# Sums of weights made during attention, each load and first add tied to a converted weight unit by a one-column Pool operation

## The chip, the core and the metric

The kernel runs on one core of one Trainium2 chip. The metric is the device time of one execution in microseconds (us); before the change its median is 2242.68 us in three runs.

## What is computed

Two layers of a transformer trunk, over 256 tokens of 2048 features, in float32. Each layer mixes the tokens with two groups of heads that read the same `x`, adds and normalises, and then runs a SwiGLU network with 5632 hidden features:

```
proj = x @ w_in                      # 5008 columns, split into qa, ka, va, qi, wi, ki, cq, ckv, kr
out_a = top-64 sparse attention(rope(qa), rope(ka), va), keys chosen by an indexer on qi, ki, wi
out_b = latent attention(rms(cq) @ w_uq, rms(ckv) @ w_ukv, rope(kr))
x = layer_norm(ALPHA * x + concat(out_a, out_b) @ w_o) * ln1_g + ln1_b
h = silu(x @ w_gate) * (x @ w_up)
x = layer_norm(ALPHA * x + h @ w_down) * ln2_g + ln2_b
```

## The kernel before

**Weights.** Nearly all of the work of TensorE (PE) is float32 products with weights, which come from HBM in units of 128 x 1024 numbers (512 KB; block TB's have 800 columns in place of 1024). SyncE (SP) issues the load of a unit into a tile `raw` (L309, four buffers in the attention phase). `parts` then makes two halves of it that together hold the full precision: ScalarE (ACT) copies it to `wh` in the rounded format (L327), VectorE (DVE) takes the difference `wl` (L328), and the buffers of `wh` and `wl` come round every five units. PE multiplies 12 times with a unit of 1024 columns, in L349, L350 and L351: two tiles of tokens, two slices of 128 rows, three products each.

**Stages of a layer.** First the blocks of the input projection, eight units each: QI0, TA, QI1, TB, then KA0, with the indexer running beside them; the latent queries (2 + 4 units), QA0, VA0, 4 units, KA1, QA1, VA1, and the output projection `w_o` (24 units, then a last pass). Attention heads are worked off between the units. Then comes the network: eleven chunks of 512 hidden features, of which the later ones multiply by a scheme with seven products in place of eight and need sums of weight units.

**Sums made ahead.** For the chunks 4 to 10 one set of these sums is made during attention, by the generator `presums`. For each chunk it loads four units into tiles `q` (four buffers) through the queue of GpSimd (Pool, L761), and DVE makes four adds and subtractions of them (L770, L771, L773, L774). The four results go back to HBM through Pool's queue (L779), from where the network stage reads them. `presums` runs once a layer, and is spawned after block TB.

**What sets the order.** The code is written as generators that say after how many ticks they go on: `tick` is called after nearly every weight unit. From the code's order a scheduler then makes one list of instructions for each engine; an operation that nothing holds back can stand in that list far ahead of its place in the code. Engines and DMA queues work strictly in the order of their lists, and wait with semaphores for each other. From the spawn of `presums` to the end of the 24 units of `w_o` there are 82 ticks, and `finish(early)` behind them runs off what is left of it.

**Other users of Pool's queue.** At the start of a layer the norm of TB's outputs uses it: the loads of `gq` and `gk` (L602, L603), and small operations `rve` and `rrs` (L585, L587) of which DVE waits in `rn` (L588). The phase after attention reuses the memory of `q`, so the first load of that phase waits for all stores of the sums.

Of the kernel before, what the change touches and what calls it, by code (L numbers as in the profile page):

```python
# [24 lines left out]
F32 = mybir.dt.float32  # L25
# [3 lines left out]
ALU = mybir.AluOpType  # L29
# [3 lines left out]
P = 128  # L33
# [49 lines left out]
def hybrid_trunk(ctx: ExitStack, tc: tile.TileContext, x, xt_in, pos, w_in, g_cq, g_ckv, w_uq,  # L83
                 w_ukv, w_o, ln1_g, ln1_b, ln1_T, w_gu, w_down, ln2_g, ln2_b, ln2_T, out):
    nc = tc.nc
# [7 lines left out]
    def nm(s):  # L93
        uid[0] += 1
        return f"{s}{uid[0]}"
# [16 lines left out]
    def pt(shape, dt, s, tag=None, bufs=1):  # L112
        assert phase["name"] == "att"
        return phase["pool"].tile(shape, dt, name=nm(s), tag=tag or s, bufs=bufs)
# [36 lines left out]
    def f(ap):  # L151
        return ap.bitcast(F32)
# [20 lines left out]
    mhalf = const.tile([P, 1], F32, name="mhalf")  # L173
# [22 lines left out]
    def rope_tables():  # L196
# [14 lines left out]
        magic = 1.5 * 2.0 ** 23  # L211
        two_pi = 2.0 * math.pi
        parts, rest = [], two_pi
        for bits in (8, 8, 8):
            e = math.floor(math.log2(rest)) + 1 - bits
# [82 lines left out]
    def some(key, have, more):  # L298

        if phase["name"] == "more":  # L300
            phase[key] = phase.get(key, 0) + 1
            if phase[key] * more % (have + more) < more:
                return phase["pool"], more
        return sb, have
# [7 lines left out]
    def load_sum(a, b):  # L312
# [3 lines left out]
        nc.gpsimd.dma_start(raw, b, accum_op=ALU.add)  # L316
        return raw

    def parts(raw, n, own=None):

        if own is not None:
            wh, wl = own[:, 0], own[:, 1]
        else:
            pool, bufs = some("n", UNITS, MORE)
            wh = pool.tile([P, KU * C], F32R, name=nm("wh"), tag="wh", bufs=bufs)
            wl = pool.tile([P, KU * C], F32R, name=nm("wl"), tag="wl", bufs=bufs)
        nc.scalar.activation(wh[:, :n], raw[:, :n], AF.Copy)  # L327
        nc.vector.tensor_tensor(wl[:, :n], raw[:, :n], f(wh[:, :n]), op=ALU.subtract)  # L328
        return wh[:, :n].rearrange("p (k c) -> p k c", k=KU), wl[:, :n].rearrange("p (k c) -> p k c", k=KU)

    def load_unit(src, n):

        return parts(load_raw(src, n), n)
# [188 lines left out]
    def layer(l, xh, xl, norms, last):  # L522
# [231 lines left out]
        def presums():  # L754

            for fc in range(ALLFROM, NFC):
                u = EARLY

                def load(i, v):
                    d = pt([P, KU * C], F32, "q", bufs=4)  # L760
                    nc.gpsimd.dma_start(d, w_gu[i][l, fc, v])  # L761
                    return d

                b12, b22 = load(1, u), load(1, u + HALF)
                yield 1
                b11 = load(0, u)
                yield 1
                b21 = load(0, u + HALF)
                yield 3
                nc.vector.tensor_tensor(b12, b12, b22, op=ALU.add)  # L770
                nc.vector.tensor_tensor(b11, b12, b11, op=ALU.add)  # L771
                yield 1
                nc.vector.tensor_tensor(b22, b11, b22, op=ALU.subtract)  # L773
                nc.vector.tensor_tensor(b21, b11, b21, op=ALU.add)  # L774
                yield 1
                ready[fc] = {}
                for i, (name, v) in enumerate((("p7", b12), ("p6", b11), ("p5", b22), ("p4", b21))):
                    d = hbm.tile([P, KU * C], F32, name=nm("q"), tag=f"{l}_{fc}_{name}", bufs=1)
                    nc.gpsimd.dma_start(d, v)  # L779
                    ready[fc][name] = d  # L780
                    if i % 2:
                        yield 2

        def aff(c):
            if l:
# [29 lines left out]
        if l == 0:  # L815
            load_x()
        early = spawn(presums())
        ka, p_ka = dsa_qk(KA0)
        finish(p_tb)
# [38 lines left out]
        def last_pass(unit, ks, lhs, then):  # L858

            us = []  # L860
            two = many([P, 2, 2, KU * C])
            for c in range(D // C):
                own = two[:, c] if c < 2 else t8([P, 2, KU * C], F32R, "own")
                us.append([load_unit(unit(c, ks[0]), KU * C), parts(load_raw(unit(c, ks[1]), KU * C), KU * C, own)])
            for t in range(NT):
                for c in range(D // C):
                    o = acc()
                    for i, k0 in enumerate(ks):
                        wh, wl = us[c][i]
                        for j in range(KU):  # L870
                            h, lo = lhs(t, k0 + j)
                            mm(o, h, wh[:, j, :], start=i == 0 and j == 0, stop=False)
                            mm(o, h, wl[:, j, :], start=False, stop=False)
                            mm(o, lo, wh[:, j, :], start=False, stop=i == len(ks) - 1 and j == KU - 1)
                        tick()
                    sl = xt[t][:, c * C:(c + 1) * C]
                    with tc.high_priority(offset=SOON):
                        nc.vector.tensor_tensor(sl, sl, o, op=ALU.add)
                then(t)
# [320 lines left out]
```

## Time and profile before

| | before |
|---|---|
| runs (3) | 2241.27 to 2244.99 us, median 2242.68 |
| the profiled execution | 2243.01 us; span 2241.2 us, mean granted clock 0.984 |
| PE busy | 2153.5 us (96%) |
| DVE busy | 1848.8 us (82%) |
| ACT busy | 1292.5 us (58%) |
| Pool busy | 215.0 us (10%) |
| DMA | 552.97 MB, mean 247 GB/s |

The time of the profiled execution is 1.8 us longer than its span, the stretch from the first to the last profiled instruction. A stretch A:B is given in us from the start of the span. In a list of operations the columns are start, duration, engine, line, operation, tiles written<-read, shape; in square brackets is the idle time of the engine just before and what ended it. "issue" there means that nothing in the profile shows what was waited for. Matmuls are pipelined, so that the durations of neighbours overlap: the distance of their starts, not their duration, is what one costs. PEclk is the share of full clock granted to PE. The lines of a helper (L309, L327 and so on) gather all its callers.

### The profile page before, as it was taken

Reading aid. Unit: us, or ns where it says so; the run is one execution under the profiler, and the core shown is the slowest. Engines: PE = TensorE matmul, PEld = TensorE weight load, DVE = VectorE, ACT = ScalarE, POOL = GpSimd, SP = SyncE. Lnnn points to the kernel's source line nnn. Section 1 sums busy time; section 2 is a strip of 40 time slices with the busy share of each in tenths; the row PEclk is TensorE's granted clock in tenths of the full one; section 3 lists DMA queues with packets and bytes.
Section 4 is the critical chain, followed back from the end, with each engine's and each line's share of the span. In section 5 each row is a group of like instructions: output and inputs, shape, how many; then the busy total and the mean of one; then the engine's idle time right before and its main releaser. Section 6 shows DMA issues by size and latency. Waiting matters only on the chain.

```text
span 2241.2 us, 28348 instructions
## 1 busy us (share of the span) xinstructions
PE 2153.5 (96%) x9948; PEld 1779.4 (79%) x9948; DVE 1848.8 (82%) x2361; ACT 1292.5 (58%) x1675; POOL 215.0 (10%) x368
## 2 busy tenths in 40 slices
PE   7869999999999999999997799999999999999997
PEld 5758888888888878878886688888888888878886
DVE  5578556799989999999666876668999899999996
ACT  4345545466666666667453455545656666666663
POOL 2220000000011010000112200000000101101101
PEclk9989999999999999999998899999999999999999
DMA  9976546667888998987759865585678889889894
GB/s 313 377 269 214 162 157 228 200 214 231 244 244 267 275 280 270 281 274 243 243 216 345 296 203 170 185 264 173 220 255 234 244 275 270 268 264 281 274 321 125
DMA packets 158833, 552.97 MB, mean 247 GB/s; under 512 B 17905, under 2 KB 18209, under 8 KB 158049
## 3 DMA queue, kind: packets, MB, share of 16 engines
q1 hardware_dynamic: 119808, 431.15, 55.4%
q0 software_dynamic: 38736, 119.87, 21.1%
q8 instruction: 78, 1.28, 0.2%
q14 instruction: 67, 0.54, 0.1%
q10 hardware_dynamic: 144, 0.13, 0.0%
HBM read 498.12 MB, written 31.46 MB: 236 GB/s over the span
## 4 chain that ended last, share of the span: by engine, by line
PE 72%; issue 9%; DVE 9%; DMA 8%; POOL 1%; ACT 1%; POOLq 0%; DVEq 0%; ACTq 0%
PE acc L350 14%; PE acc L349 14%; PE acc L351 14%; DVE wl L328 4%; PE gu_p L971 4%; PE gu_p L972 4%; PE gu_p L969 4%; DMA raw<-in_w_up_dram 3%; PE gu_c L972 2%; PE gu_c L969 2%; PE gu_c L971 2%; PE tr L369 2%; DMA q<-q 2%; DMA q<-in_w_up_dram 2%; PE att L972 1%
## 5 line engine op out<-in xcount | busy, mean ns | idle before, releaser
L327 ACT ACTIVATE wh<-raw 128x1024 fp32r<-128x1024 f32 (+1 forms) x910 | 939.5, 1054 | 683.6 <-PE acc L351 247.3
L328 DVE TENSOR_TENSOR wl<-raw,wh 128x1024 fp32r<-128x1024 f32 (+1 forms) x910 | 1079.6, 1214 | 217.7 <-ACT wh L327 213.4
L349 PE MATMUL acc<-wh,xh 128*128 128x512 f32 (+1 forms) x768 | 307.4, 401 | 6.8 <-ACT wh L327 6.7
L350 PE MATMUL acc<-wl,xh 128*128 128x512 f32 (+1 forms) x768 | 302.4, 394 | 9.1 <-DVE wl L328 9.1
L351 PE MATMUL acc<-wh,xl 128*128 128x512 f32 (+1 forms) x768 | 301.4, 393 | 0.0
L350 PE MATMUL acc<-wl,hT 128*128 128x512 f32 x640 | 250.5, 391 | 0.4
L349 PE MATMUL acc<-wh,hT 128*128 128x512 f32 x640 | 249.4, 390 | 0.0
L351 PE MATMUL acc<-wh,hT 128*128 128x512 f32 x640 | 249.3, 390 | 0.0
L349 PEld LDWEIGHTS acc<-wh,xh 128*128 128x128 f32 x768 | 147.8, 192 | 39.7 <-ACT wh L327 8.9
L350 PEld LDWEIGHTS acc<-wl,xh 128*128 128x128 f32 x768 | 147.6, 192 | 39.2 <-DVE wl L328 13.0
L351 PEld LDWEIGHTS acc<-wh,xl 128*128 128x128 f32 x768 | 147.2, 192 | 28.8 <-DVE xl L415 0.6
L350 PEld LDWEIGHTS acc<-wl,hT 128*128 128x128 f32 x640 | 120.1, 188 | 29.8 <-DVE wl L328 5.3
L349 PEld LDWEIGHTS acc<-wh,hT 128*128 128x128 f32 x640 | 120.2, 188 | 25.2
L969 PE MATMUL gu_c<-wh,xh 128*128 128x512 f32 x360 | 140.2, 389 | 0.0
L972 PE MATMUL gu_c<-wh,xl 128*128 128x512 f32 x360 | 140.1, 389 | 0.0
L971 PE MATMUL gu_c<-wl,xh 128*128 128x512 f32 x360 | 140.1, 389 | 0.0
L351 PEld LDWEIGHTS acc<-wh,hT 128*128 128x128 f32 x640 | 120.2, 188 | 24.5
L316 POOL DMA_DIRECT2D sum<-in_w_up_dram x56 | 47.9, 855 | 902.0 <-DMA sum<-in_w_up_dram 414.7
L1082 POOL DMA_DIRECT2D x<-d x80 | 68.8, 891 | 488.8 <-ACT d L1081 478.4
L971 PE MATMUL gu_p<-wl,many 128*128 128x512 f32 x240 | 94.6, 394 | 7.5 <-DVE wl L328 7.5
L972 PE MATMUL gu_p<-wh,many 128*128 128x512 f32 x240 | 93.5, 390 | 0.0
L969 PE MATMUL gu_p<-wh,many 128*128 128x512 f32 x240 | 93.5, 389 | 0.0
(294 smaller groups left out, 3680.3 us busy)
## 6 DMA issues: line engine op xcount, KB each, us to landing
raw<-in_w_gate_dram SPq DMA_DIRECT2D x176, 512.0 KB, 6.5
raw<-in_w_down_dram SPq DMA_DIRECT2D x176, 512.0 KB, 7.9
raw<-in_w_in_dram SPq DMA_DIRECT2D x144, 512.0 KB, 4.6
raw<-in_w_up_dram SPq DMA_DIRECT2D x106, 512.0 KB, 5.5
raw<-in_w_o_dram SPq DMA_DIRECT2D x64, 512.0 KB, 4.6
q<-q POOLq DMA_DIRECT2D x56, 512.0 KB, 5.5
sum<-in_w_up_dram SPq DMA_DIRECT2D x56, 512.0 KB, 3.7
sum<-in_w_up_dram POOLq DMA_DIRECT2D x56, 512.0 KB, 8.7
```

Source lines behind the costliest of these rows:

```text
L316: nc.gpsimd.dma_start(raw, b, accum_op=ALU.add)
L327: nc.scalar.activation(wh[:, :n], raw[:, :n], AF.Copy)
L328: nc.vector.tensor_tensor(wl[:, :n], raw[:, :n], f(wh[:, :n]), op=ALU.subtract)
L349: mm(o[t][:, :n], h, a, start=first, stop=False)
L350: mm(o[t][:, :n], h, b, start=False, stop=False)
L351: mm(o[t][:, :n], l, a, start=False, stop=final)
L369: nc.tensor.transpose(psum[:, i * P:(i + 1) * P], s, ident)
L969: mm(o[name], h, a, start=name not in begun, stop=False)
L971: mm(o[name], h, b, start=False, stop=False)
L972: mm(o[name], l, a, start=False, stop=end)
L1082: nc.gpsimd.dma_start(xt[t][:, c * C:(c + 1) * C], d, accum_op=ALU.add)
```

## The change

Three things change, in `parts`, `presums` and a new helper.

- `parts` remembers the `wh` tile that it last handed out (`latest["wh"]`).
- Ahead of each load of `presums`, a Pool operation writes the first column of the tile to be loaded, from the first column of that `wh`. The load overwrites the tile afterwards; so it has to wait for the operation, and the operation for the conversion of that unit.
- Ahead of the first add of each chunk, a Pool operation reads the first columns of `b12` and of the latest `wh` into a small tile `gate`. The add overwrites `b12`, and so has to wait for it.

The waits of the generator change by one tick: 4 in place of 3 between the last load and the first add, 1 in place of 2 after each pair of stores. A chunk takes 10 ticks in place of 11, 70 in place of 77 for the seven chunks. The first column values that are written are overwritten by the loads; the sums and their results stay the same.

```diff
+    latest = {}
+
+    def not_until_now(*tiles):
+        for v in tiles:
+            nc.gpsimd.tensor_tensor(v[:, 0:1], mhalf, f(latest["wh"][:, 0:1]), op=ALU.add)
+
     def parts(raw, n, own=None):
...
+        latest["wh"] = wh
         nc.scalar.activation(wh[:, :n], raw[:, :n], AF.Copy)
...
                 def load(i, v):
                     d = pt([P, KU * C], F32, "q", bufs=4)
+                    not_until_now(d)
                     nc.gpsimd.dma_start(d, w_gu[i][l, fc, v])
                     return d
...
                 b21 = load(0, u + HALF)
-                yield 3
+                yield 4
+                gate = pt([P, 1], F32, "gate", bufs=2)
+                nc.gpsimd.tensor_tensor(gate, b12[:, 0:1], f(latest["wh"][:, 0:1]), op=ALU.add)
                 nc.vector.tensor_tensor(b12, b12, b22, op=ALU.add)
...
                     if i % 2:
-                        yield 2
+                        yield 1
```

In the changed file the lines behind `parts` have numbers 9 to 12 higher: L327 and L328 become L336 and L337, the loads L761 become L771, the adds L770 to L774 become L782 to L786, the stores L779 become L791. The new ties are L325 and the gates L781.

The instruction lists show where the operations stand. First Pool's list near the start of the program, before; `q_1032` to `q_1090` are the four tiles of the first chunk, `gbT` are gains of the norms.

```order
L203 DMA pos_i<-in_pos_dram 128x2x1
L761 DMA q_1032<-in_w_up_dram 128x1024
L761 DMA q_1034<-in_w_up_dram 128x1024
L761 DMA q_1070<-in_w_gate_dram 128x1024
L761 DMA q_1090<-in_w_gate_dram 128x1024
L200 MEMSET rope_288 128x1 x48
L420 DMA gbT_3529<-in_ln_T_dram 128x32
```

The same place after the change; `wh_953` is the last unit of block TB, `wh_1043` and `wh_1077` are the first two of KA0.

```order
L200 MEMSET rope_288 128x1 x48
L325 TENSOR_TENSOR q_1032<-mhalf,wh_953 128x1 [waits Activation_49]
L325 TENSOR_TENSOR q_1035<-mhalf,wh_953 128x1
L771 DMA q_1032<-in_w_up_dram 128x1024 [waits Pool_49]
L771 DMA q_1035<-in_w_up_dram 128x1024 [waits Pool_49]
L325 TENSOR_TENSOR q_1072<-mhalf,wh_1043 128x1 [waits Activation_49]
L771 DMA q_1072<-in_w_gate_dram 128x1024 [waits Pool_49]
L325 TENSOR_TENSOR q_1093<-mhalf,wh_1077 128x1 [waits Activation_49]
L771 DMA q_1093<-in_w_gate_dram 128x1024 [waits Pool_49]
L611 DMA gq_969<-in_g_cq_dram 128x512 [waits DMAHW4_49,DVE_49]
L612 DMA gk_970<-in_g_ckv_dram 128x256 [waits DMAHW0_49,DMASW0_49,PE_49]
```

The loads of the first chunk stood ahead of everything that waits; now each stands behind a tie that waits for ACT, and the first two wait for the last unit of TB. Second, DVE's list around the first add of the first chunk, before; `wl_169` and `wl_193` belong to the fourth and fifth units of the program's first block, and `xl` are the halves of `x` made there.

```order
L328 TENSOR_TENSOR wl_169<-raw_166,wh_168 128x1024 [waits DMAHW7_49,Activation_49]
L373 TENSOR_TENSOR xl_70<-xs_184,xh_68 128x256 [waits DMAHW0_49,Activation_49]
L373 TENSOR_TENSOR xl_71<-xs_184,xh_69 128x256 [waits Activation_49]
L770 TENSOR_TENSOR q_1032<-q_1032,q_1034 128x1024 [waits DMASW2_49,DMASW1_49]
L328 TENSOR_TENSOR wl_193<-raw_190,wh_192 128x1024 [waits DMAHW1_49,Activation_49]
```

The same add after the change; `wl_1207` is of the sixth unit of KA0, `score` is the indexer's, `rn` the norm's.

```order
L597 SCALAR_TENSOR_TENSOR rn_1022<-cq_396,rrs_1027,gq_969 128x512 [waits Activation_49,Pool_49]
L337 TENSOR_TENSOR wl_1207<-raw_1204,wh_1206 128x1024 [waits DMAHW7_49,PE_49]
L654 SCALAR_TENSOR_TENSOR score_823<-rel_1064,wi_394,score_823 128x256 [waits Activation_49]
L782 TENSOR_TENSOR q_1032<-q_1032,q_1035 128x1024 [waits DMASW4_49,DMASW3_49]
L654 SCALAR_TENSOR_TENSOR score_823<-rel_1066,wi_394,score_823 128x256 [waits DVE_49,Activation_49]
L783 TENSOR_TENSOR q_1072<-q_1032,q_1072 128x1024 [waits DMASW5_49,DVE_49]
```

The first add has moved from the fifth unit of block QI0 to behind the sixth of KA0. Third, Pool's list where the norm of TB's outputs stands in it, after the change; `wh_1206` is that sixth unit.

```order
L594 TENSOR_SCALAR rve_1009<-ss_1007 128x1 [waits Activation_49]
L596 TENSOR_TENSOR rrs_1011<-rve_1009,mhalf 128x1 [waits Pool_49]
L781 TENSOR_TENSOR gate_1222<-q_1032,wh_1206 128x1 [waits DMASW3_49,Activation_49]
L594 TENSOR_SCALAR rve_1017<-ss_1015 128x1 [waits Activation_49]
L596 TENSOR_TENSOR rrs_1019<-rve_1017,mhalf 128x1 [waits Pool_49]
```

Before, loads and stores of the seventh chunk stood among these operations (among them the one below); now it is the first chunk's gate, with half of the norm's operations behind it.

```order
L585 TENSOR_SCALAR rve_1009<-ss_1007 128x1 [waits Activation_49]
L761 DMA q_3202<-in_w_up_dram 128x1024 [waits DMASW5_49,DMASW4_49]
L587 TENSOR_TENSOR rrs_1011<-rve_1009,mhalf 128x1 [waits Pool_49]
L585 TENSOR_SCALAR rve_1017<-ss_1015 128x1 [waits Activation_49]
L587 TENSOR_TENSOR rrs_1019<-rve_1017,mhalf 128x1 [waits Pool_49]
```

## The prediction

> **What bounds the kernel now.** First the profile's page, whose slices of 56 us say where TensorE (PE) is not busy.
>
> ```profile
> PE   7869999999999999999997799999999999999997
> GB/s 313 377 269 214 162 157 228 200 214 231 244 244 267 275 280 270 281 274 243 243 216 345 296 203 170 185 264 173 220 255 234 244 275 270 268 264 281 274 321 125
> ```
>
> PE is full except in the first three slices, in slices 22 and 23 (about 1160 to 1290 us) and at the end. The first two places are the starts of the two layers, and the DMA rate is highest there. Next the table by stretches (columns: length; busy time of PE, PEld, DVE, ACT, POOL; granted clock; DMA share; GB/s).
>
> ```profile
> 0.00:40.00 40.00, 30.86 (x118) 23.07 (x119) 23.13 (x40) 18.92 (x29) 9.05 (x68) 1.00 0.93 330
> 40.00:80.00 40.00, 27.80 (x109) 21.81 (x107) 26.84 (x60) 16.71 (x25) 7.45 (x14) 0.87 0.94 349
> 80.00:120.00 40.00, 36.03 (x184) 31.86 (x185) 22.55 (x33) 14.39 (x21) 9.60 (x18) 0.91 0.96 353
> 120.00:160.00 40.00, 24.63 (x108) 19.13 (x107) 28.09 (x64) 14.84 (x32) 9.78 (x19) 0.79 0.78 273
> 160.00:240.00 80.00, 80.00 (x428) 67.38 (x427) 62.65 (x142) 43.62 (x69) 3.82 (x7) 1.00 0.61 203
> 240.00:330.00 90.00, 90.00 (x476) 76.32 (x475) 52.78 (x107) 47.88 (x87) 0.00 (x0) 1.00 0.49 157
> 330.00:440.00 110.00, 110.00 (x509) 91.41 (x508) 75.21 (x109) 52.50 (x78) 2.86 (x4) 1.00 0.69 225
> 600.00:1000.00 400.00, 395.63 (x1756) 324.43 (x1756) 373.41 (x348) 266.86 (x291) 37.56 (x44) 1.00 0.88 269
> 1160.00:1200.00 40.00, 31.09 (x130) 25.12 (x129) 22.89 (x33) 12.55 (x18) 9.04 (x17) 0.87 0.94 351
> 1200.00:1240.00 40.00, 35.21 (x195) 30.65 (x194) 25.20 (x42) 16.87 (x26) 8.62 (x17) 0.91 0.92 334
> 1240.00:1280.00 40.00, 26.26 (x120) 20.84 (x120) 34.08 (x81) 16.96 (x31) 12.95 (x23) 0.83 0.80 282
> ```
>
> To 160 us PE idles 40.7 of 160 us, and 27.4 of 120 us after 1160, with DMA at 0.8 to 0.96 of its time; from 160 to 440 us it never idles, at 157 to 225 GB/s. Why it idles there is seen where a wait ends, in the order of time, first PE, then DVE (start, duration, operation, idle time before it).
>
> ```profile
> 28.38 0.39 PE L349 MATMUL acc<-wh,xh 128*128 128x512 f32 x1
> 48.10 0.39 PE L349 MATMUL acc<-wh,xh 128*128 128x512 f32 x1
> 53.32 0.79 PE L350 MATMUL acc<-wl,xh 128*128 128x512 f32 x1 [4.15 <-DVE wl L328]
> 53.91 0.63 PE L351 MATMUL acc<-wh,xl 128*128 128x512 f32 x1
> 57.75 0.63 PE L351 MATMUL acc<-wh,xl 128*128 128x512 f32 x1
> ```
> ```profile
> 44.27 0.25 DVE L235 SCALAR_TENSOR_TENSOR rope<-rope 128x96 f32<-128x96 f32 x1
> 50.74 1.23 DVE L770 TENSOR_TENSOR q<-q,q 128x1024 f32<-128x1024 f32 x1 [6.22 <-issue]
> ```
>
> DVE had nothing to do from 44.5 to 50.74 us because its next instruction is the first add of a weight sum (L770), whose operands were still under way; the `wl` that PE needs stands behind it in DVE's queue. So PE stops for 4.15 us. It also starts slowly after that: 87 matmuls lie between the starts at 28.38 and 48.10, or 0.227 us apart, but 9 between 53.91 and 57.75, or 0.43 apart. The waits of DVE, in sum:
>
> ```profile
> DVE q L770 <- issue: 46.9, 8, 7.9
> DVE q L770 <- DMA q<-in_w_up_dram: 19.3, 3, 10.2
> ```
>
> DVE stands 66.2 us at this one add, 11 times. Weights for PE come late too: the answers on DMAs give the median time to landing, first for 60 to 150 us, then for 240 to 330.
>
> ```profile
> raw<-in_w_in_dram SPq DMA_DIRECT2D x12, 512.0 KB, 7.3
> ```
> ```profile
> raw<-in_w_in_dram SPq DMA_DIRECT2D x22, 512.0 KB, 3.7
> ```
>
> **What the change moves.** The loads and stores of the sums, and their number:
>
> ```profile
> L761 POOL DMA_DIRECT2D q<-in_w_up_dram x28: 532/533/603, 2.7 to 1278.8; - x28
> L761 POOL DMA_DIRECT2D q<-in_w_gate_dram x28: 527/533/602, 3.7 to 1283.6; - x28
> q<-q POOLq DMA_DIRECT2D x56, 512.0 KB, 5.5
> DMA to landing us min/median/max: 2.9/6.9/13.9
> ```
>
> That is 28 loads and 28 stores a layer of 0.524 MB, 29.4 MB. Now they start at 2.7 us; with the change none starts before the last unit of block TB is converted, and then eight DMAs go with ten ticks, a tick being nearly always one weight unit. Nothing is computed less: the same DMAs and the same 28 adds and subtractions a layer, and 70 Pool operations more.
>
> *First layer, 0 to 160 us.* The time that PE's work there takes at full pace comes from the groups of that stretch (one line of the three alike; each of L349, L350, L351 issues one per k):
>
> ```profile
> L349 PE MATMUL acc<-wh,xh 128*128 128x512 f32 x113 | 47.8, 425 | 6.8 <-ACT wh L327 6.7
> L349 PE MATMUL acc<-wh,xh 128*128 128x400 f32 x32 | 11.9, 372 | 0.0
> 6.06 1.22 PE L349 MATMUL acc<-wh,xh 128*128 128x512 f32 x2 [6.06 <-ACT wh L327]
> ```
>
> 339 matmuls of 512 columns by 0.227 are 76.9 us; 96 of 400 columns, by 0.227 x 400/512 = 0.177, are 17.0; for the small rest I estimate 5. With 6.1 us before the first matmul and 2 us of slow first ones (about 10, each 0.2 late) that is 107; 53 of the 160 us are lost. What stays lost I can only bound. The norm of TB's outputs is a chain through Pool and DVE that does not vanish, and the ropes and the indexer have waits of their own: I let 10 us stay, so the term is -43; bounds -50 (3 stay) and -30 (23 stay, for instance if the 15 us that PE idles after 120 us are that chain's own).
>
> *Second layer, 1160 to 1280 us.* Its groups:
>
> ```profile
> L349 PE MATMUL acc<-wh,xh 128*128 128x512 f32 x83 | 33.8, 407 | 0.0
> L349 PE MATMUL acc<-wh,xh 128*128 128x400 f32 x32 | 11.4, 357 | 0.0
> ```
>
> 249 of 512 columns are 56.5 us, the 96 short ones 17.0, and the rest I estimate at 6: 80 of 120 us, 40 lost. I let 7 stay: -33, bounds -38 and -22.
>
> *Where the DMAs go.* From 160 to 440 us the table's rates make 80 x 203 + 90 x 157 + 110 x 225 = 55 MB. With up to 29.4 more that is at most 84 MB in 280 us, 300 GB/s (some of it is there already, and the last ticks end before 440, which about cancel). The nearest stretch with PE full is 600 to 1000 us: 269 GB/s, 1.1% idle. At that idle share the term is 3 us a layer. The rate asked for is above that row's and below the 353 that a crowded stretch reached, so I take +4 a layer, +8 in all, between 0 and +20 a layer (the stage held to 280 GB/s: 84/0.280 = 300 us).
>
> *The new operations.* A tie reads one column of the last `wh` and writes one column of the tile to be loaded. The nearest operations are the norm's, on Pool, and what DVE did at the second one's time:
>
> ```profile
> 142.57 0.18 POOL L585 TENSOR_SCALAR rve<-ss 128x1 f32<-128x1 f32 x1 [3.05 <-ACT rn L583]
> 149.72 0.75 POOL L585 TENSOR_SCALAR rve<-ss 128x1 f32<-128x1 f32 x1
> ```
> ```profile
> 149.67 0.75 DVE L588 SCALAR_TENSOR_TENSOR rn<-cq,rrs,gq 128x512 f32<-128x512 f32 x1 [0.89 <-POOL rrs L587]
> ```
>
> 0.18 us alone, 0.75 beside a DVE operation that ran from 149.67 for 0.75. So a tie costs 0.2 to 1.4 us (a DVE add of 1.23 ahead of it): 70 are 14 to 98 us of a queue that is busy for 215 of 2241 us, and no PE work waits on Pool as such. Term 0. [...]
>
> *What is queued behind a tie.* On Pool, the next loads and, at the first chunk, half of the norm's small operations behind a gate on the sixth unit of KA0. That unit's slot is free once KA0's first unit is through PE, some 3 us into KA0, and the transposes that need the norm come three units in, after 8 us: cover 5 us, price a stall of a few us a layer, inside the 10 and 7 that I let stay. On DVE, the first add now also waits for the gate; the unit whose conversion opens it is converted just ahead of the add, and five units of `wh` (5 x 12 x 0.227 = 13.6 us) stand ready for PE. On ACT, a conversion waits until a tie has read the slot it overwrites, five units on. On SP, the first load of the next phase waits, as before, for every store of the sums; the last ones now land only shortly ahead of it. Four raw units and five converted ones are ahead of PE then, 24 us by the same pace, against 5.5 us for a store: +1 a layer, bounds 0 and +7 (half of the longest landing, 13.9). In the second layer the loads of the last norm's gains stand on Pool among the sums, and DVE waits for them a landing of some 5 us at most, with the same units ahead of PE: nothing.
>
> Sum: -43 - 33 + 8 + 2 = -66. The profiled execution took 2243.0 us for a span of 2241.2; that is 0.3 above the median of 2242.7, so the forecast is 2177 against either. Its own range: -50 - 38 = -88 gives 2155, and -30 - 22 + 20 gives 2211.
>
> **The rivals.**
>
> *The queue of the DMAs only moves.* At full pace ten units of 2.72 us ask for 10 + 8 DMAs of 0.524 MB, 347 GB/s, just what the crowded stretches gave. Attention's small matmuls lie between the units and stretch the ticks, which speaks against it; that there are only four raw buffers in this phase speaks for it, and so does the split of 60 to 150 us (packets, MB, share):
>
> ```profile
> q1 hardware_dynamic: 3436, 12.66, 35.7%
> q0 software_dynamic: 5158, 18.70, 57.8%
> ```
>
> While Pool's queue was full SP got 141 GB/s. If SP gets half of the 349 of 40 to 80 us while Pool's is busy, 175, a unit takes 3.0 us, not 2.72: over 70 units +20 a layer, +40 in place of +8, 2209. [...]
>
> *The stalls are the stage's own.* Only DVE's waits at L770 go, and half of their 66.2 us reaches PE: -33, 2210. Against it: PE's 4.15 us and slow start above follow from one such wait.
>
> *Slower.* A tie on a sum's tile waits for the store of that tile's old content; ACT's conversion five units later waits for the tie. If stores took longer than those 13.6 us, ACT would stop, and PE with it, once in each of 14 chunks. To undo the 66 us it must cost over 4.7 each, so stores of over 18.3 us; the longest DMA of these tiles took 13.9, at the most crowded time. At 21 us it would be 14 x 7.4 = 104 against 66: 2281.
>
> *It does not hold.* If the loads went ahead of their place all the same, the time would stay at 2243; the order shows them behind their ties.
>
> **How the numbers follow.** Forecast 0.76; the queue only moves 0.12; the stage's own stalls 0.06; slower 0.03; no effect 0.03. The time is the first one's, 2177. The range, 2155 to 2211, is its own, with the two middle cases at its upper end. 0.2% is 4.5 us, about what a measurement of this kernel can tell from no change: faster 0.94, same 0.03, slower 0.03.
>
> **What would show it.** Right: from 20 us on PE is full at clock 1.00 in the first layer, and again from 1160; the DVE waits at the first add fall from 66 us below 15; the early landing of `raw` falls to about 4 us; GB/s fall to about 200 in the first slices and rise to 250 to 300 in those from 160 to 400 us; the end of the first layer moves by about 38 us. Wrong: PE idle spread through the attention stage with `raw` landings over 7 us (first rival), PE waiting at `att` or the ropes at the old places (second), or ACT waiting for Pool's ties (third).

## The result, and the profile after

The changed kernel takes 2170.5 us (median of four runs, 2169.07 to 2172.17), beside 2243.8 us for the kernel before (four runs): a ratio of 0.967 with a 95% interval of [0.9651, 0.969], 73 us less. The profiled execution took 2169.3 us for a span of 2167.5. The prediction said 2177, between 2155 and 2211. One run of kernel 7 below took 5700 us and is left out of its median. The kernels below were timed in several series, each beside the kernel before, and the median of that kernel lay between 2240.9 and 2243.8 us in them; so a few us between two kernels of different series tell little by themselves, and there the traces are compared.

The page of the changed kernel, slices of 54 us, busy tenths of PE and DMA rate:

```profile
PE   8999999999999999999999999999999999999997
GB/s 301 205 294 274 295 288 286 175 204 243 262 255 264 284 262 266 280 279 248 212 150 226 295 291 272 311 261 179 205 251 258 269 264 271 283 254 272 285 316 116
```

The two dips at the layers' starts are gone, and the DMA rate no longer has its peak there. Then the table by stretches (length; busy PE, PEld, DVE, ACT, POOL; granted clock; DMA share; GB/s); the second layer starts about 46 us earlier than before, so that 1150 to 1230 us here is what was 1196 to 1276 us there.

```profile
0.00:40.00 40.00, 33.89 (x139) 27.48 (x140) 30.23 (x70) 25.79 (x40) 4.88 (x60) 1.00 0.84 288
40.00:80.00 40.00, 40.00 (x185) 33.80 (x183) 20.16 (x39) 17.88 (x25) 0.00 (x0) 1.00 0.65 218
80.00:120.00 40.00, 40.00 (x234) 33.74 (x234) 33.66 (x74) 24.69 (x45) 15.08 (x25) 1.00 0.72 260
120.00:160.00 40.00, 39.15 (x225) 33.42 (x224) 39.45 (x98) 22.84 (x36) 9.11 (x19) 1.00 0.84 299
160.00:240.00 80.00, 80.00 (x418) 68.13 (x418) 55.04 (x97) 42.43 (x74) 17.76 (x29) 1.00 0.79 288
240.00:330.00 90.00, 90.00 (x442) 74.84 (x441) 65.68 (x115) 45.74 (x80) 21.17 (x30) 1.00 0.81 288
1150.00:1190.00 40.00, 40.00 (x237) 34.20 (x236) 33.09 (x73) 24.37 (x45) 12.60 (x22) 1.00 0.72 248
1190.00:1230.00 40.00, 39.81 (x223) 33.99 (x221) 39.55 (x93) 21.28 (x36) 9.38 (x18) 1.00 0.82 289
```

PE idles 7.0 of the first 160 us, 6.1 of them ahead of the first matmul, where it idled 40.7 before, and the granted clock is 1.00 in all these stretches. From 160 to 330 us DMA rises from 157 to 203 GB/s to 288, and PE stays full. No wait of DVE at the first add (now L782) is left in the trace; before it was 66.2 us. How much each layer gained is read from one operation that stands in both layers' network stage, the product with the sums' operands (count: min/median/max ns, first and last start in us), before:

```profile
L969 PE MATMUL gu_p<-wh,many x240: 387/389/398, 495.5 to 2162.7; 128*128 128x512 f32 x120
```

and after:

```profile
L981 PE MATMUL gu_p<-wh,many x240: 387/389/398, 449.6 to 2088.8; 128*128 128x512 f32 x120
```

Its first start, in the first layer, comes 45.9 us earlier; its last, in the second layer, 73.9. So the first layer gained 45.9 us and the second 28.0.

### The profile page after: what moved, and what is told of

It is laid out like the page before. It is cut to its first block, busy times and chain, and to the rows that moved or that the text cites. A ratio compares the mean times of both kernels' runs of the same rounds, so it can differ in the third digit from the quotient of the medians.

```text
span 2167.5 us, 28478 instructions
## 1 busy us (share of the span) xinstructions
PE 2138.0 (99%) x9948; PEld 1769.1 (82%) x9948; DVE 1850.9 (85%) x2361; ACT 1291.1 (60%) x1675; POOL 267.1 (12%) x438
## 4 chain that ended last, share of the span: by engine, by line
PE 77%; DVE 11%; issue 5%; DMA 5%; ACT 1%; POOL 0%; DVEq 0%; POOLq 0%; ACTq 0%; SPq 0%
PE acc L359 17%; PE acc L358 17%; PE acc L360 17%; DVE wl L337 6%; DMA raw<-in_w_up_dram 4%; PE gu_p L983 3%; PE gu_p L984 3%; PE gu_p L981 3%; PE tr L378 2%; PE gu_c L981 2%; PE gu_c L984 2%; PE gu_c L983 2%; PE att L983 1%; PE att L981 1%; PE att L984 1%
## 5 line engine op out<-in xcount | busy, mean ns | idle before, releaser
L336 ACT ACTIVATE wh<-raw 128x1024 fp32r<-128x1024 f32 (+1 forms) x910 | 939.2, 1054 | 635.0 <-PE acc L360 248.5
L337 DVE TENSOR_TENSOR wl<-raw,wh 128x1024 fp32r<-128x1024 f32 (+1 forms) x910 | 1080.4, 1216 | 215.1 <-ACT wh L336 210.4
L359 PE MATMUL acc<-wl,xh 128*128 128x512 f32 (+1 forms) x768 | 297.7, 388 | 0.0
```

The lines of the kernel that those rows point to most:

```text
L359: mm(o[t][:, :n], h, b, start=False, stop=False)
```

## The experiments

Ten kernels. Each diff is against the changed kernel where nothing else is said, and `...` stands for lines left out. Each ratio is to the kernel before, timed in the same series.

**1. No gates.**

```diff
-                gate = pt([P, 1], F32, "gate", bufs=2)
-                nc.gpsimd.tensor_tensor(gate, b12[:, 0:1], f(latest["wh"][:, 0:1]), op=ALU.add)
```

> The changed kernel without its 14 gates; loads tied as in the change. In DVE's list the first add of the first chunk now stands behind the 33rd weight unit of the program, where the changed kernel has it behind the 38th and the kernel before behind the 4th. Theory A (the gain comes from both sides of the pair, the loads held back and DVE freed of waiting at the first add): the add now comes about as its operands land, so DVE waits again, some 2 to 5 us in each of 14 chunks, 30 to 70 us in all, but PE has up to five converted units ahead and loses only part of it: 2180 us, 2172 to 2195. Theory B (only the crowding of the DMAs at the layers' starts mattered, the waits of DVE did not): 2171 us, within 3 of the changed kernel, whatever DVE waits. Theory C (the waits of DVE were all of it): 14 waits of 3 to 5 us give back half or more of the 73 us: 2205 to 2220.

Measured: 2219.0 us, a ratio of 0.9894 [0.9871, 0.9917]. Two thirds of the gain are gone. The waits of DVE (line L780 is the first add here, L781 and L784 the next ones), and the landing of `raw` from 60 to 150 us:

```profile
DVE q L780 <- DMA q<-in_w_up_dram: 45.9, 12, 7.5
DVE q L781 <- DMA q<-in_w_gate_dram: 15.1, 5, 5.4
DVE q L780 <- DMA q<-in_w_gate_dram: 13.8, 2, 6.9
```
```profile
raw<-in_w_in_dram SPq DMA_DIRECT2D x13, 512.0 KB, 5.6
```

The queues are as uncrowded as in the changed kernel (5.6 us to landing, there 5.3), but DVE waits 88 us in all at the sums (smaller groups of 7.2, 5.2 and 1.0 us are not shown), more than before the change, when it was 71. 48 us of time for 88 us of waiting: about half of it reaches PE. The time is theory C's; that these waits were all of the loss before the change, as C had it, does not follow, and kernel 6 speaks against it. A, with its five converted units ahead of PE, was too kind by 39 us. The longest waits of PE say why:

```profile
PE tr L378 <- ACT qk L543: 9.2, 2, 6.9
PE tr L378 <- DVE lg L497: 8.6, 4, 4.3
PE att L644 <- ACT rel L649: 8.5, 2, 4.4
```

The longest waits are not for `wl`. PE waits for the softmax (`lg`), the heads (`qk`) and the indexer (`rel`), small operations of DVE and ACT that stand behind the add; of these nothing is made ahead.

**2. No ties.**

```diff
                     d = pt([P, KU * C], F32, "q", bufs=4)
-                    not_until_now(d)
                     nc.gpsimd.dma_start(d, w_gu[i][l, fc, v])
```

> The changed kernel without its 56 ties on the loads; the gates stay. The first adds stand at the same units in DVE's list as in the changed kernel (38, 48, 58 ...), the first four loads go at the program's start again, and every later load goes as soon as the store of its tile's old sum has landed. Theory A (a gate holds the whole chain, since the stores follow the adds and the next loads follow the stores, so that only four loads, 2.1 MB, stay at the start): DVE waits at the first add below 10 us in all, and 2171 us, 2167 to 2178. Theory B (each load has to be held back by itself): the crowding returns in part, raw landings of 6 us or more from 60 to 150 us, 2190 us or more.

Measured: 2171.55 us, 0.9687 [0.9669, 0.9704]: the whole gain, with 14 of the 70 new operations. Theory A. The landing of `raw` from 60 to 150 us is lower still, and Pool's loads (L770 here) now wait for the stores of their tiles:

```profile
raw<-in_w_in_dram SPq DMA_DIRECT2D x15, 512.0 KB, 4.4
```
```profile
POOL q L770 <- DMA q<-q: 99.9, 34, 7.1
```

There are four tiles; a load that is due early waits for a store, a store for its add, and the add for the gate. One gate per chunk holds the whole chain. The ties are not needed where gates are.

**3. Ties and gate for the first chunk alone** (both behind `if fc == ALLFROM`).

```diff
-                    not_until_now(d)
+                    if fc == ALLFROM:
+                        not_until_now(d)
...
-                gate = pt([P, 1], F32, "gate", bufs=2)
-                nc.gpsimd.tensor_tensor(gate, b12[:, 0:1], f(latest["wh"][:, 0:1]), op=ALU.add)
+                if fc == ALLFROM:
+                    gate = pt([P, 1], F32, "gate", bufs=2)
+                    nc.gpsimd.tensor_tensor(gate, b12[:, 0:1], f(latest["wh"][:, 0:1]), op=ALU.add)
```

> The changed kernel with ties and gate only at the first of the seven chunks. In DVE's list the first adds of a layer stand behind the units 38, 42, 50, 55, 59, 64, 67, where the changed kernel has 38, 48, 58, 68, 78, 88, 98: the other six chunks follow as fast as loads, adds and stores let them. Theory A (a wait of DVE at the first add and crowded queues cost PE time wherever they are): DVE waits again 20 to 50 us in all, at some 120 to 300 us and 1270 to 1420 us, and PE loses there; 2195 us, 2183 to 2215. Theory B (the start of a layer is the only place where it costs, since the norm of block TB and the ropes are chained there): 2171 us, within 4 of the changed kernel.

Measured: 2224.3 us, 0.9919 [0.9899, 0.9938]; the interval of theory A is missed by 9 us, on the side that makes its reason stronger. The layers' starts are as good as after the change, and the loss has moved behind them. The stretch from 160 to 240 us, the waits of DVE at the first add (L784), and one of them in the order of time:

```profile
160.00:240.00 80.00, 62.00 (x303) 52.45 (x304) 52.05 (x95) 34.61 (x63) 17.61 (x33) 0.88 0.90 328
```
```profile
DVE q L784 <- DMA q<-in_w_up_dram: 58.1, 11, 8.7
```
```profile
234.62 1.23 DVE L784 TENSOR_TENSOR q<-q,q 128x1024 f32<-128x1024 f32 x1 [7.86 <-DMA q<-in_w_up_dram]
235.76 0.35 DVE L497 TENSOR_SCALAR lg<-lg,rc 128x256 f32<-128x256 f32 x1
236.17 1.33 PE L378 MATMUL tr<-ident,lg 128*128 128x128 f32 x5 [6.81 <-DVE lg L497]
```

DVE waits 7.86 us for a load; the softmax's scaling (L497) stands behind the add, and PE, which needs it next, idles 6.81 us. So it is not the place in the layer: where the sums run as fast as loads allow, PE pays. The queues are crowded there too (328 GB/s in this stretch, 288 in the changed kernel), so these 54 us are not those of the waits alone.

**4. The old ticks.**

```diff
-                yield 4
+                yield 3
...
                     if i % 2:
-                        yield 1
+                        yield 2
```

> The changed kernel with the waits of the kernel before: 3 and 2 ticks in place of 4 and 1, a chunk in 11 ticks. The first adds stand behind the units 37, 48, 59 ... 103, where the changed kernel has 38, 48, 58 ... 98. Theory A (the ticks matter little once loads and adds are tied to them): 2171 us, within 4 of the changed kernel; one tick less between the last load and the first add may bring DVE waits of 1 to 2 us a chunk. Theory B (the four ticks between the last load and the first add are what keeps DVE from waiting): DVE waits of over 30 us at the first add and 2185 us or more. Theory C (the later end delays the first load of the phase after attention): a gap of PE of up to 7 us near 440 and 1480 us, 2176 to 2182.

Measured: 2171.7 us, 0.9687 [0.9669, 0.9704]. Theory A: the ticks make no difference that can be measured.

**5. The norm off Pool's queue,** against the kernel before.

```diff
-            nc.gpsimd.tensor_scalar(ve, ss, 1.0 / n, RMS_EPS, ALU.mult, ALU.add)
+            nc.vector.tensor_scalar(ve, ss, 1.0 / n, RMS_EPS, ALU.mult, ALU.add)
...
-            nc.gpsimd.tensor_tensor(rs, ve, mhalf, op=ALU.pow)
+            nc.vector.reciprocal(ve, ve)
+            nc.scalar.activation(rs, ve, AF.Sqrt)
...
-            nc.gpsimd.dma_start(gq, g_cq[l].partition_broadcast(P))
-            nc.gpsimd.dma_start(gk, g_ckv[l].partition_broadcast(P))
+            nc.sync.dma_start(gq, g_cq[l].partition_broadcast(P))
+            nc.sync.dma_start(gk, g_ckv[l].partition_broadcast(P))
```

> The kernel before (no ties, no gates), with the norm of block TB's outputs taken off Pool: the mean of squares and its reciprocal on VectorE, the root on ScalarE, the loads of its gains through SyncE's queue. Loads and adds of the sums stand as before. In the profile of before the two longest idle times of PE are 11.82 us (until 152.84) and 13.74 us (until 1258.96), and at both a load of the sums stands in Pool's queue between the norm's operations and waits 4.75 and 3.30 us for a store of the sums to land. Theory A (Pool's order, stores and loads of the sums ahead of the norm's operations, makes a good part of these two gaps): both gaps shrink to under 6 us and the time falls by 12 to 25 us, to 2218 to 2231. Theory B (the gaps are the wait of VectorE at the first add, or the stage's own chain): the gaps stay and the time is 2236 to 2248.

Measured: 2236.8 us, 0.9976 [0.996, 0.9993], 5 us less. The time is theory B's. The two gaps did shrink, from 11.82 and 13.74 us to 6.49 and 8.77, not to under 6 as theory A had it, and they now end with the norm's results on DVE (`rn`). The longest waits of PE, the third number being the longest single one:

```profile
PE tr L369 <- DVE rn L589: 15.3, 2, 8.8
PE tr L369 <- DVE hd L260: 12.0, 2, 7.6
PE tr L369 <- DVE dup L558: 10.6, 2, 8.9
```

These are norm, heads and ropes on DVE, whose longest waits at the adds here are 8.8 and 6.5 us; the waits for heads and ropes stood at 5.8 and 7.6 us in the kernel before. In the second layer's gap DVE waited 3.18 us for a load at the first add, just ahead of `rn`. Pool's order was a wait that ended last in these gaps, and others stood right behind it.

**6. Crowded queues alone:** 32 more loads a layer that nobody reads.

```diff
+        for i in range(32):
+            d = pt([P, KU * C], F32, "q", bufs=4)
+            nc.gpsimd.dma_start(d, w_gu[i % 2][l, 3, i % 4])
         early = spawn(presums())
```

> The changed kernel with 32 loads more in each layer, 16.8 MB, through Pool's queue into the four tiles q ahead of the first tie; nobody reads them, so VectorE waits for none of them. They crowd the DMA queues at the start of a layer as before the change, without a wait at an add. Theory A (the waits of VectorE at the first adds, and what stands behind them, were the cost; a crowded queue costs little by itself): raw landings of about 7 us up to 90 us, DMA share above 0.9, and PE loses up to 5 us a layer: 2176 us, 2171 to 2183. Theory B (the crowded queues were themselves the cost): PE loses some 20 us a layer in that stretch as before the change: 2200 to 2215.

Measured: 2199.8 us, 0.981 [0.9784, 0.9836], 29 us more than the changed kernel, with no wait of DVE at any add. Theory A is out, and B's 2200 is nearly reached, but not with 20 us in each layer: by the first and last starts of the same product as above (473.0 and 2117.6 us), the first layer loses 23.4 us and the second 5.4. The two layers differ, in the stretches of the first 80 us and of 1150 to 1190:

```profile
0.00:40.00 40.00, 27.32 (x92) 18.43 (x93) 18.91 (x41) 16.48 (x26) 12.78 (x75) 1.00 0.97 379
40.00:80.00 40.00, 32.46 (x135) 26.08 (x133) 20.42 (x44) 17.44 (x24) 9.02 (x17) 0.91 1.02 419
1150.00:1190.00 40.00, 40.00 (x220) 35.38 (x218) 23.41 (x48) 19.38 (x28) 10.07 (x19) 1.00 1.03 415
```

In the first 80 us PE idles 20.2 us, before the change 21.3, after it 6.1. What ACT waited there for `raw` (10 to 80 us), in the kernel before, in this one, and in the changed one:

```profile
ACT wh L327 <- DMA raw<-in_w_in_dram: 29.6, 15, 6.2
```
```profile
ACT wh L336 <- DMA raw<-in_w_in_dram: 23.6, 11, 5.0
```
```profile
ACT wh L336 <- DMA raw<-in_w_in_dram: 1.9, 6, 0.5
```

So at the program's start late weights alone can cost as much as was lost there before. But these queues are fuller than before the change: 379 and 419 GB/s, there 330 and 349, and a `raw` asked for from 10 to 40 us lands after 13.3 us and from 40 to 80 us after 8.0, there 7.5 and 7.4. How much of the old loss was the crowd is therefore not shown. At the second layer's start the same crowd, 415 GB/s, costs PE nothing up to 1190 us, while the kernel before idled there. The one large gap of PE in this kernel's second layer, 9.0 us, stands behind a load of the norm's gains, which comes behind the 32 in Pool's queue:

```profile
DVE rn L597 <- DMA gk<-in_g_ckv_dram: 8.6, 1, 8.6
```

**7. Each tie four times.**

```diff
-        for v in tiles:
+        for v in tiles * 4:
```

> The changed kernel with each tie written four times: 168 one-column operations on Pool more, at the median of 0.61 us that a tie took in the changed kernel some 100 us of Pool's time. Theory A (no work of PE waits for a tie): 2171 us, within 3 of the changed kernel. Theory B (VectorE is held while Pool reads, as Pool is held by VectorE): VectorE's operations in the attention stage get longer, its mean for wl rises above 1.22 us, and the time rises by 10 us or more. Theory C (ScalarE's conversions wait for the ties that read the slot they overwrite): ScalarE waits for ties 30 us or more in all, 7.2 us in the changed kernel, and the time rises by 3 to 15 us.

Measured: 2165.6 us (three runs), 0.966 [0.9631, 0.969]: no cost. It is 5 us less than the changed kernel, which was timed in another series, and none of the theories has that; the spans of the two traces differ by 0.5 us only. Ties and `wl` from 100 to 330 us in the changed kernel, then here (busy, mean ns):

```profile
L337 DVE TENSOR_TENSOR wl<-raw,wh 128x1024 fp32r<-128x1024 f32 x69 | 83.5, 1220 | 44.1 <-ACT wh L336 44.1
L325 POOL TENSOR_TENSOR q<-mhalf,wh 128x1 f32<-128x1 f32 x24 | 17.5, 742 | 28.9 <-ACT wh L336 21.4 <-issue 5.8 <-DMA q<-q 1.5
```
```profile
L337 DVE TENSOR_TENSOR wl<-raw,wh 128x1024 fp32r<-128x1024 f32 x69 | 83.4, 1219 | 44.2 <-ACT wh L336 44.2
L325 POOL TENSOR_TENSOR q<-mhalf,wh 128x1 f32<-128x1 f32 x96 | 33.4, 373 | 22.2 <-issue 9.5 <-ACT wh L336 8.9 <-DMA q<-q 1.8
```

72 more ties took (33.4 - 17.5) / 72 = 0.22 us each, and `wl` did not get longer. ACT waited for ties 7.2 us in all in both kernels: theories B and C fall.

**8. One set of sums.** Only the first chunk's sums are made; the other six chunks read them, so the network works on other numbers.

```diff
             for fc in range(ALLFROM, NFC):
+                if fc > ALLFROM:
+                    ready[fc] = ready[ALLFROM]
+                    continue
```

> The changed kernel with the sums of the first chunk alone made in each layer; the other six chunks of the network read those of the first in place of their own. So it leaves out 24 loads, 24 stores (25.2 MB) and 24 adds or subtractions of a layer; the network stage does the same work on other numbers. What falls away is all that the sums still cost in the changed kernel. Theory A (the forecast's terms: 4 us a layer for the DMAs moved into the attention stage and 1 us for the wait at the next phase, and little else): 2161 us, 2156 to 2167. Theory B (wholly hidden): 2170 us. Theory C (the queue only moved): 2130 us.

Measured: 2160.35 us, 0.9632 [0.9607, 0.9657], 10.2 us less than the changed kernel, timed in another series, and 5 less than kernel 7, timed in the same one. The traces give 9.8 us, not alike in the layers: the product's first start is at 446.9 us in place of 449.6, its last at 2079.0 in place of 2088.8, which is 2.7 us in the first layer and 7.1 in the second. The sum of theory A is right, but its 5 us in each layer are not: PE is also full here from 1300 to 1340 us, where the changed kernel loses some 5 us at the gains (kernel 10).

**9. The adds on Pool,** against kernel 5.

```diff
-                nc.vector.tensor_tensor(b12, b12, b22, op=ALU.add)
-                nc.vector.tensor_tensor(b11, b12, b11, op=ALU.add)
+                nc.gpsimd.tensor_tensor(b12, b12, b22, op=ALU.add)
+                nc.gpsimd.tensor_tensor(b11, b12, b11, op=ALU.add)
...
-                nc.vector.tensor_tensor(b22, b11, b22, op=ALU.subtract)
-                nc.vector.tensor_tensor(b21, b11, b21, op=ALU.add)
+                nc.gpsimd.tensor_tensor(b22, b11, b22, op=ALU.subtract)
+                nc.gpsimd.tensor_tensor(b21, b11, b21, op=ALU.add)
```

> The kernel with the norm off Pool (no ties, no gates, 2236.8 us), and with the four adds of each chunk on Pool in place of VectorE. Loads, adds and stores go as early as before, so the queues are crowded at the layers' starts, but VectorE never waits for a sum. Theory A (VectorE's waits at the adds cost most, the crowded queue the smaller part, as the 29 us of the kernel with 32 loads more say): the second layer's start loses little and the first one's some 20 us: 2190 us, 2180 to 2205. Theory B (the crowded queue costs nearly all): 2225 us or more, with raw landings over 7 us at both starts. Theory C (Pool's long adds and VectorE's operations exclude each other, so that VectorE slows down): VectorE's operations beside them take longer than in the kernel before (wl over 1.3 us in the mean up to 160 us), and the time stays above 2215 us.

Measured: 2235.1 us, 0.9973 [0.9957, 0.9989]. It was meant to take DVE's waits alone away, and does not tell. The signs of theory C came true (`wl` over 1.3 us in the mean, a time above 2215 us), and so did those of B (2225 us or more, with `raw` landing after 7.9 us from 20 to 130 us and 8.5 from 1160 to 1240). The `wl` operations up to 160 us in the kernel before, then in this one (busy, mean ns):

```profile
L328 DVE TENSOR_TENSOR wl<-raw,wh 128x1024 fp32r<-128x1024 f32 (+1 forms) x40 | 46.7, 1172 | 16.9 <-ACT wh L327 16.7
```
```profile
L328 DVE TENSOR_TENSOR wl<-raw,wh 128x1024 fp32r<-128x1024 f32 (+1 forms) x42 | 67.8, 1627 | 23.0 <-ACT wh L327 23.0
```

And in the whole program (min/median/max ns):

```profile
L328 DVE TENSOR_TENSOR wl<-raw,wh x910: 978/1217/1227, 6.0 to 2201.2; 128x1024 fp32r<-128x1024 f32 x178, 128x800 fp32r<-128x800 f32 x4
```
```profile
L328 DVE TENSOR_TENSOR wl<-raw,wh x910: 977/1220/6127, 5.8 to 2189.0; 128x1024 fp32r<-128x1024 f32 x178, 128x800 fp32r<-128x800 f32 x4
```

The mean up to 160 us rises from 1.17 to 1.63 us, and the longest is 6.1 us in place of 1.2. So how much of the second layer's loss before the change was DVE's waits with the queues crowded as they were is not shown by itself.

**10. The gains later.** In the second layer the gains of the last norm are loaded through Pool's queue among the sums; here they are applied eight ticks after their loads are asked for, behind gates of the same kind.

```diff
         def aff(c):
             if l:
-                affine(ln2_g[l - 1], ln2_b[l - 1], c)
+                gained.append(spawn(gain(c)))
+
+        gained = []
+
+        def gain(c):
+            sl = slice(c * C, (c + 1) * C)
+            gc, bc = load_gb(ln2_g[l - 1], ln2_b[l - 1], sl)
+            yield 8
+            for t in range(NT):
+                gate = pt([P, 1], F32, "gate", bufs=2)
+                nc.gpsimd.tensor_tensor(gate, xt[t][:, c * C:c * C + 1], f(latest["wh"][:, 0:1]), op=ALU.add)
+            for t in range(NT):
+                nc.vector.tensor_tensor(xt[t][:, sl], xt[t][:, sl], gc, op=ALU.mult)
+                nc.vector.tensor_tensor(xt[t][:, sl], xt[t][:, sl], bc, op=ALU.add)
...
-        finish(*a, *b)
+        finish(*a, *b, *gained)
```

> The changed kernel, with the gains of the last norm applied eight ticks after their loads are asked for, behind gates of the same kind (8 gates on Pool more, second layer only). In the changed kernel VectorE waits 3.7 us for their loads between 1290 and 1330 us, and PE loses some 7 us between 1320 and 1340 us. In VectorE's list the gains now stand three weight units later than in the changed kernel. Theory A (that wait is what holds VectorE and PE there): 2165 us, 2161 to 2168. Theory B (the place is slow for another reason, the softmax of two heads at once beside the sums): 2170 us, within 2 of the changed kernel.

Measured: 2164.85 us (five runs), 0.966 [0.9646, 0.9674]; 5.7 us less than the changed kernel, timed in another series. That time is theory A's, but it does not decide alone, since kernel 7, with the gains where the changed kernel has them, took 2165.6 us. The traces do: the product's first start is at 449.3 us in place of 449.6, its last at 2083.5 in place of 2088.8, so 5.0 us are gained in the second layer. From 1300 to 1340 us, with DVE's wait there, in the changed kernel, and then the stretch in this one:

```profile
1300.00:1340.00 40.00, 36.22 (x174) 29.12 (x173) 29.56 (x61) 17.53 (x34) 10.18 (x16) 0.96 0.78 266
```
```profile
DVE x L445 <- DMA g<-in_ln_g_dram: 3.7, 2, 2.5
```
```profile
1300.00:1340.00 40.00, 40.00 (x203) 32.85 (x203) 31.68 (x64) 20.14 (x38) 11.37 (x22) 1.00 0.89 317
```

PE gets 203 matmul records done where it had 174. How the wait reached PE in the changed kernel, in the order of time: two waits of DVE for the gains, then the softmax's scaling (`lg`), then the transpose that reads it.

```profile
1319.16 1.29 DVE L445 TENSOR_TENSOR x<-x,g 128x512 f32<-128x512 f32 x2 [2.48 <-DMA g<-in_ln_g_dram]
1322.93 1.29 DVE L445 TENSOR_TENSOR x<-x,g 128x512 f32<-128x512 f32 x2 [1.27 <-DMA g<-in_ln_g_dram]
1328.51 0.28 DVE L497 TENSOR_SCALAR lg<-lg,rc 128x128 f32<-128x128 f32 x1
1328.93 0.30 PE L378 MATMUL tr<-ident,lg 128*128 128x128 f32 x1 [3.78 <-ACT qk L543]
```

The profile puts the last wait down to `qk`; `lg`, which the transpose reads, ends just ahead of it.

## Why the prediction was right, point by point

- **The two layer starts (-43 and -33).** Right in place and nearly in size. With the other terms the forecast gave -38 for the first layer and -28 for the second; measured -45.9 and -28.0. In the first the 10 us let stay were too many: PE idles 7.0 us there, 6.1 of them ahead of the first matmul, which had been counted apart. So those 15 us were not the "chain's own", as the upper bound had it: they went with the sums. In the second layer the -28.0 holds the 5.0 us lost at the gains (below); without them it would have been -33.
- **The DMAs moved into attention (+8), the next phase's first load (+2).** Right in sum, partly by luck: what six of seven sets of sums still cost is about 10 us by the traces (kernel 8), but some 5 of them go with the gains of the last norm, which the forecast put at nothing. That leaves some 5 us where 10 were forecast for all seven; how the sums and the gains share the 10 was not tried with both taken away. The rate asked for, at most 300 GB/s, came out at 288, and PE stayed full, so the first rival is out: `raw` landed after 4.5 us (from `w_in`) and 5.2 us (from `w_o`) from 240 to 330 us, not over 7. That SP gets half of the rate while Pool's queue is busy was an estimate of the author's: SP's queue moved 40% of the bytes from 60 to 150 us before the change (12.66 of 31.36 MB) and 51% from 40 to 80 us in kernel 6 (8.48 of 16.77 MB).
- **The gains of the last norm in the second layer ("nothing").** Wrong: 5.0 us by the traces (kernel 10). The cover named was converted weight units, and DVE's wait for the gains did not stop PE through a weight unit but through the softmax behind it in DVE's queue.
- **New operations and what is queued behind a tie (0).** Right: four times as many ties cost nothing that can be measured, and no wait of PE is for Pool.
- **That waiting of DVE is covered by five units of `wh`.** This reason held in the changed kernel only since nothing waited. Where DVE did wait (kernel 1), half of it reached PE: 48 us for 88. Kernel 3 lost 54 us with 65 us of waiting (58.1 and two smaller groups of 3.8 and 3.0), with crowded queues beside it. The second rival had guessed half; it fell not by that but because the waits were not the only cost, as kernel 6 says.
- **What would show it.** PE full at clock 1.00 and no wait at the first add: as said. `raw` landing: 5.3 us, not 4. The rates of the first three slices: 301, 205 and 294, not 200 each; the first of them holds no sums at all, since the first tie starts at 83 us. The first layer ended 46 us earlier, not 38.
- **The range.** Its upper end, 2211, is narrower than the prediction's own bounds: it takes +20 once where the bound is +20 a layer, and leaves out the +7 a layer for the next phase's first load. All upper bounds together, -30 - 22 + 40 + 14, give 2245. The measured 2170.5 lies well below both.

Two causes stand behind the 73 us, and the prediction had priced them as one. Waits of DVE without crowded queues cost 48 us (kernel 1, for 88 us of waiting; the 66 us before the change would be 36 at that rate, which is an estimate). Crowded queues without such waits cost 23 us in the first layer (kernel 6, with queues fuller than before the change); the 5 us of its second layer hang on the load behind the 32. At the program's start the crowd alone can cost what was seen before, though how it and the waits shared the loss is not shown. At the second layer's start it does not, which leaves the waits of DVE and Pool's order behind them; how these two share it stays open as well.

## What to carry to other kernels

Work made ahead for a later stage must be held back where it takes part in in-order queues: a scheduler that hoists an operation to the front of an engine's list makes all that is behind it wait for its operands, as DVE did here for 66.2 us at the first adds. Hold the consumer, not only the load: one gate per chunk on the first add was enough, since loads and stores followed it round the four tiles, while ties on the loads alone kept a third of the gain (kernels 2 and 1: 2171.55 and 2219.0 us). And ask of each cover what PE reads next: converted weights ahead of it did not help where its next instruction needed a softmax (6.81 us of PE for 7.86 us of DVE in kernel 3).

## What the runs showed of the hardware

In these traces the matmuls behind a stop of PE of a few us start further apart at first, so that it costs more than its length. In kernel 1, after an idle time of 4.42 us, in the order of time:

```profile
112.41 2.08 PE L644 MATMUL att<-kiT,qiT 64*128 64x256 f32 x8 [4.42 <-ACT rel L649]
...
116.39 0.63 PE L359 MATMUL acc<-wl,xh 128*128 128x512 f32 x1
116.82 0.63 PE L360 MATMUL acc<-wh,xl 128*128 128x512 f32 x1
...
118.44 0.39 PE L358 MATMUL acc<-wh,xh 128*128 128x512 f32 x1
118.67 0.39 PE L359 MATMUL acc<-wl,xh 128*128 128x512 f32 x1
```

The large matmuls start 0.43 us apart up to 118.10, and 0.23 apart from 118.44 on. From 112.41 to 118.44 are 6 us; if all the work in them went at that pace, some 3 us were lost on top of the 4.42, which is an estimate from the two distances.

The granted clock says the same in the kernel before. At the stop of 4.15 us that ends at 53.32 it falls to 0.50 at 51.42, while PE still stands, and is back at 1.00 at 58.25; the large matmuls start 0.43 us apart up to 58.18, and 0.23 apart from 58.46 on. Behind its first matmul that trace has nine stops of PE of 2.40 to 13.74 us, and with each a stretch at 0.50, of 3.4 us (for instance from 116.27 to 119.69), 6.8 (from 51.42 to 58.25), 10.2 (from 1181.23 to 1191.47) or 13.7 us (from 143.58 to 157.23).

DVE's operations got longer beside Pool's long ones. With adds on Pool of 2.4 to 2.9 us (medians), single `wl` operations took up to 6.1 us in place of 1.2 (kernel 9), while the short ties did not lengthen the mean at all (1.220 and 1.219 us, kernel 7). Some rows of kernel 9, in the order of time:

```profile
59.44 1.23 DVE L328 TENSOR_TENSOR wl<-raw,wh 128x1024 fp32r<-128x1024 f32 x1 [1.41 <-ACT wh L327]
60.54 2.40 POOL L771 TENSOR_TENSOR q<-q,q 128x1024 f32<-128x1024 f32 x1 [4.29 <-DMA q<-in_w_up_dram]
61.97 2.05 DVE L328 TENSOR_TENSOR wl<-raw,wh 128x1024 fp32r<-128x1024 f32 x1 [1.30 <-ACT wh L327]
63.05 3.22 POOL L772 TENSOR_TENSOR q<-q,q 128x1024 f32<-128x1024 f32 x1
64.48 10.70 DVE L328 TENSOR_TENSOR wl<-raw,wh 128x1024 fp32r<-128x1024 f32 x4 [0.46 <-ACT wh L327]
66.82 2.80 POOL L774 TENSOR_TENSOR q<-q,q 128x1024 f32<-128x1024 f32 x1
69.59 3.38 POOL L775 TENSOR_TENSOR q<-q,q 128x1024 f32<-128x1024 f32 x1
```

The `wl` at 59.44 us, which shares only its last 0.13 us with the add at 60.54, took 1.23 us; the one at 61.97, which begins beside that add, 2.05; the four from 64.48 on, beside three adds, 10.70 together, or 2.7 each.
